# Reordering the prologue of a decoder-trunk kernel: condition weights in four staging places, three first row tiles' products beside them

## The chip, the cores and the metric

The kernel runs on one core of a Trainium2 chip. The metric is the device time of one execution in microseconds; lower is better. It is given as the median of several runs. One execution was also recorded by the hardware profiler, and every row shown below comes from that one.

## What is computed

One inference step of a one-layer decoder trunk, for 1024 prompt tokens and 8 sample tokens, width 1024. What matters here is the beginning:

```python
mod = (silu(c) @ w_ada + b_ada)              # six shifts, scales and gates per batch row
h = rmsnorm(x, g_mix) * (1.0 + sc_m) + sh_m  # needs scale and shift of mod
z = h @ w_in                                 # 256 + 4*768 columns: u | q | k | v | gate
```

Behind it stand causal pooling over u, multi-scale retention over six heads of q, k, v, an output projection, a gated MLP with a short convolution, and a final norm. All data are float32.

## The kernel before

**Tiles.** The 1024 channels lie in 8 blocks of 128 partitions (index k or j). The 1032 tokens lie in the free dimension and are cut into three row tiles c = 0, 1, 2 of 384, 384 and 264 columns (the last holds the eight samples). The normed and modulated input h is kept as a pair h_hi, h_lo, and each w_in column block as a pair hi, lo, so that one block product takes three matmuls for each k: 24 for all eight.

**The prologue** is made of small named operations, and ORDER is a list that says in which order the program emits them. An operation whose inputs have not been emitted is passed over until they are. The names:

- `L{j}{half}` loads a 512 KB block of the condition weights w_ada for channel block j (16 of them); `M{j}{half}` multiplies it by silu(c) on TensorE (four products, eight records); `F{j}` transposes the result and writes scale and shift of block j on VectorE (L257 to L263).
- `l{i}` loads the w_in column block i of the first five (q, k, v of head 0, q, k of head 1), `w{i}` splits it into hi (ScalarE, L220) and lo (VectorE or GpSimd, L221).
- `X{c}{i}` loads half of row tile c of x (that of c = 0, called x0 in the text, is loaded ahead of the list); `q{c}{k}` squares block k, with the sum `s{c}{k}` onto acc (L502); `S{c}` adds over partitions on TensorE (L302) and takes the power -1/2 on GpSimd (L292), `r{c}` spreads it over the partitions (L311) and copies it to R (L319).
- `h{c}{k}` modulates block k of row tile c: a product on VectorE (L366), or on ScalarE and GpSimd (L363, L364), then h_hi on ScalarE (L367) and h_lo on VectorE (L368). `hs` does it for the samples (L375 to L380).
- `p{c}{k}` adds block k's share to the row tile's products z in PSUM (L339 to L341): five column blocks for c = 0, two for c = 1.
- `i` begins the stream of the later weights through a ring of three raw buffers, which l0 to l4 also use.

ENG says for each such name which engine does it (0 VectorE, 1 GpSimd, for squares 2 ScalarE). A load without a place of its own in `spots` uses the raw ring: before, that is j = 5. Three staging places of two blocks each lie in memory that the h tiles of row tiles 1 and 2 use later; j = 3, 6 follow j = 0 in the first, 4 and 7 follow 1 in the second, and 2 has the third.

All these loads are issued by SyncE, one queue in order: a load that waits for its buffer holds up those behind it. The framework that builds the program puts the instructions of each engine in order itself and starts from the list's order; each engine then runs its own in order.

**After the prologue** the main loop goes through the remaining products of the input projection. Its first one, v of head 0 for row tile 1, needs a PSUM bank that the evacuation of q (head 0, row tile 0; L595 to L597) sets free, as all eight are taken.

Of the kernel before, what the change touches and what calls it, by code (L numbers as in the profile page):

```python
# [11 lines left out]
F32 = mybir.dt.float32  # L12
# [5 lines left out]
P = 128  # L18
D = 1024
KT = D // P  # L20
# [11 lines left out]
LEN = (384, 384, 264)  # L32
# [49 lines left out]

ENG = {'w3': 0, 's23': 0, 'q21': 0, 's02': 0, 's27': 0, 's12': 1, 'q20': 2, 'q12': 0, 'w2': 0, 's22': 0, 's20': 0, 't02': 1, 'q01': 2, 's17': 0, 'q13': 2, 'e': 2, 'q15': 1, 's24': 1, 's03': 0, 's16': 1, 'q05': 1, 's11': 0, 's21': 1, 't05': 0, 's15': 1, 't15': 1, 's25': 1, 'q27': 1, 'q07': 2, 't21': 1, 'q24': 2, 't16': 1, 'q10': 2, 's14': 1, 'q06': 2, 's05': 1, 't10': 0, 's06': 0, 'q26': 0, 'q11': 1, 'q04': 0, 'q00': 2, 'q02': 2, 's10': 0, 't17': 1, 's04': 1, 'q17': 2, 't13': 0, 's07': 1, 'q25': 1, 'q14': 2, 'q22': 2, 'q23': 0, 'q16': 2, 's13': 0, 't06': 0, 'q03': 2, 's26': 0, 's01': 1, 't20': 0, 'w0': 0, 't03': 0, 't24': 0, 't22': 1, 't26': 1, 'w1': 1, 's00': 0}
ORDER = """
q00 q05 l0 p00 l1 L10 L01 L00 L11 p03 q02 q03 M31 L21 l2 p04 q01 r0 h13 q07
q06 h01 S0 L20 l3 l4 X11 X10 L50 M01 p01 q15 S1 w1 L31 h26 q12 w0 M11 h25
M00 F5 L40 F0 q16 h24 L41 q04 i w2 L30 L51 q14 h00 w3 F2 M10 F1 M20 h02
M21 F3 w4 p10 p02 M30 q13 M50 M51 q21 M71 M40 q22 q11 p12 q10 h23 L60 q17 X20  # L90
h07 L61 h03 M70 p15 h15 p13 q20 M41 p11 X21 M61 h14 h20 L70 p14 h05 F4 q26 r1
M60 L71 h10 h17 h06 p05 q23 r2 p17 h04 F6 q24 h11 h22 S2 F7 q25 h16 h12 q27
p06 p16 h27 p07 hs h21
""".split()


# [33 lines left out]
def trunk_step(  # L130
# [40 lines left out]
    act = rights.enter_context(tc.tile_pool(name="act", bufs=1, side="right", reuse_waits="tile"))  # L171
# [3 lines left out]
    def big(name, dt=F32):  # L175
        return tp.tile([P, TS], dt, tag="t", name=name)

    def bank(name):
        return pg.tile([P, 512], F32, tag="g", name=name)
# [18 lines left out]
    def chunk_tile(c, tag, name, dt=F32):  # L198
        return act.tile([P, KT, LEN[c]], dt, tag=f"{tag}{c}", name=f"{name}{c}")
# [8 lines left out]
    def load_raw(src, name, raw=None):  # L208
        if raw is None:
            raw = wp.tile([P, 1024], F32, tag="raw", name=f"raw_{name}", bufs=NRAW)  # L210
        if isinstance(src, list):
            for i, part in enumerate(src):
                nc.sync.dma_start(raw[:, i * 512:(i + 1) * 512].rearrange("p (k c) -> p k c", k=2), part)
        else:
            nc.sync.dma_start(raw, src)
        return raw
# [119 lines left out]
    def gemm_k(ps, n, w, k, xh, xl, first, last):  # L336
        hi, lo = w
        ws = slice(k * P, (k + 1) * P)
        mm(ps[:, 0:n], hi[:, ws], xh[:, k, 0:n], start=first, stop=False)  # L339
        mm(ps[:, 0:n], hi[:, ws], xl[:, k, 0:n], start=False, stop=False)  # L340
        mm(ps[:, 0:n], lo[:, ws], xh[:, k, 0:n], start=False, stop=last)  # L341

    def gemm(ps, n, w, xh, xl):
        for k in range(KT):
            gemm_k(ps, n, w, k, xh, xl, k == 0, k == KT - 1)
# [10 lines left out]
    hh = [chunk_tile(0, "hh", "h_hi", F32R)]  # L356
    hl = [chunk_tile(0, "hl", "h_lo", F32R)]

    def modulate(dh, dl, src, c, k, R, scale, shift, name, spread=False):
        np_ = PLEN[c]  # L360
        t = big(name)[:, 0:np_]
        if spread:
            nc.scalar.activation(t, src[c][:, k, 0:np_], AF.Copy, scale=scale[:, k, 0:1])  # L363
            nc.gpsimd.tensor_tensor(t, t, R[:, 0:np_], op=ALU.mult)  # L364
        else:
            nc.vector.scalar_tensor_tensor(t, src[c][:, k, 0:np_], scale[:, k, 0:1], R[:, 0:np_], ALU.mult, ALU.mult)  # L366
        nc.scalar.activation(dh[c][:, k, 0:np_], t, AF.Identity, bias=shift[:, k, 0:1])  # L367
        nc.vector.scalar_tensor_tensor(  # L368
            dl[c][:, k, 0:np_], t, shift[:, k, 0:1], dh[c][:, k, 0:np_].bitcast(F32), ALU.add, ALU.subtract)
# [23 lines left out]
    for bi in range(len(in_blocks)):  # L393
        if bi < HEADS:
            for _ in range(2 if bi == 0 else 6):
                p, j, half = todo.pop(0)
# [7 lines left out]
    ready = {}  # L404
# [16 lines left out]
    def weight(key):  # L421
        while key not in ready:
            split_next()
        return ready[key]


    first = [m for (_, _, m) in in_blocks[0] + in_blocks[1]][0:NFIRST]
    early = (first, first[0:ENG.get("e", 1)])
    stage = [act.tile([P, 2, 1024], F32, tag=t, name=f"stage_{t}") for t in ("hh2", "hl2", "hl1")]
    spots = {0: stage[0], 1: stage[1], 2: stage[2], 3: stage[0], 4: stage[1], 6: stage[0], 7: stage[1]}  # L430
    ada_raw, ada_bank = {}, {}
    zps = {}
    R1, acc1, part1 = {}, {}, {}

    ops = {}
    DVE, GPS = nc.vector, nc.gpsimd
    on = lambda name, default: (DVE, GPS)[ENG.get(name, default)]

    def def_load(j, half):
        def fn():  # L440
            spot = spots[j][:, half] if j in spots else None
            ada_raw[j, half] = load_raw(w_ada[2 * j + half], f"ada0_{j}_{half}", spot)
        prev = [i for i in spots if i < j and spots[i] is spots.get(j)]
        ops[f"L{j}{half}"] = [f"M{i}{half}" for i in prev], fn

    def def_mm(j, half):
        def fn():
# [14 lines left out]
    for j in range(KT):  # L462
        for half in range(2):
            def_load(j, half)
            def_mm(j, half)
        def_fin(j)
# [20 lines left out]
    def def_sq(c, k):  # L487
        n = LEN[c]

        def fn():  # L490
# [3 lines left out]
            else:  # L494
                d = big(f"sq1_{c}_{k}")[:, 0:n]
            e = ENG.get(f"q{c}{k}", 2)
            if e == 2:
# [10 lines left out]
    def def_h(c, k):  # L508
        def fn():
            while len(hh) <= c:  # L510
                hh.append(chunk_tile(len(hh), "hh", "h_hi", F32R))
                hl.append(chunk_tile(len(hl), "hl", "h_lo", F32R))
            if ENG.get(f"t{c}{k}"):
                modulate(hh, hl, xt, c, k, R1[c], scale1, sh_m, f"h1t{c}_{k}", True)
            else:
                modulate(hh, hl, xt, c, k, R1[c], scale1, sh_m, f"h1t{c}_{k}")
        deps = [f"F{k}", f"r{c}"]
        if c == 1:
            deps += ["M20", "M21"]
        if c == 2:  # L520
            deps += ["M70", "M71", "M60", "M61", "h10"]
        ops[f"h{c}{k}"] = deps, fn

    def def_part(c, k):
        def fn():
            for m in early[c]:
                if (m, c) not in zps:
                    zps[m, c] = bank(f"z{m}_{c}")
                gemm_k(zps[m, c], LEN[c], ready["in", m], k, hh[c], hl[c], k == 0, k == KT - 1)
        deps = [f"h{c}{k}"] + [f"w{i}" for i in range(len(early[c]))]  # L530
        if k == KT - 1:
            deps += [f"p{c}{i}" for i in range(KT - 1)]
        elif k:
            deps.append(f"p{c}0")
        ops[f"p{c}{k}"] = deps, fn

    def set_acc(c):
        part1[c] = rms_a(acc1[c], c, "n1")
# [4 lines left out]
    for c in range(3):  # L543
        if c:
            def_x(c)
        for k in range(KT):
            def_sq(c, k)
            def_h(c, k)
            if c < 2 and early[c]:
                def_part(c, k)  # L550
        ops[f"S{c}"] = [f"q{c}{k}" for k in range(KT)], lambda c=c: set_acc(c)
        ops[f"r{c}"] = (f"S{c}",), lambda c=c: set_R(c)
# [5 lines left out]
    while todo_ops:  # L558
        name = next(n for n in todo_ops if all(d in done for d in ops[n][0]))
# [283 lines left out]
    for bi, blk in enumerate(in_blocks):  # L843
        g = 0
        if bi == len(in_blocks) - 1:
# [12 lines left out]
            w0 = e1p.tile([P, 2, 1024], F32R, tag="e", name="w_o0")  # L858
            split2(w0, raw)
            wo = {0: [(w0[:, 0, i * 512:(i + 1) * 512], w0[:, 1, i * 512:(i + 1) * 512]) for i in range(2)]}  # L860
        for c in range(3):
            for kind, i, m in blk:
# [3 lines left out]
                if new:  # L866
                    w = weight(("in", m))
# [381 lines left out]
    for i, (m, t) in enumerate(tail):  # L1249
# [3 lines left out]
        if i < NLEAD:  # L1253
            f = FSEQ[i]
# [43 lines left out]
    for k in (4, 5, 6, 7, 0, 1, 2, 3):  # L1298
# [7 lines left out]
        else:  # L1306
            h11, h12, h22 = x2[k, 0], x2[k, 1], x2[k + 4, 1]
# [172 lines left out]
    for p, (wn, bn) in enumerate(OUT_PRODS[:-1]):  # L1480
        ps = [banks(f"o{p}_{m}") for m in range(4)]
        st = None
        for k in range(FH - NLATE):
# [4 lines left out]
            if (p, k) in XLOADS:  # L1488
                m, t = XLOADS[p, k]
# [147 lines left out]
```

## Time and profile before

| | |
|---|---|
| median of three runs | 1235.36 us (1233.45 to 1235.67) |
| profiled execution, its own time | 1235.19 us |
| its span, first to last instruction | 1233.4 us |
| mean granted clock of TensorE | 0.986 of full speed |
| TensorE busy | 1196.7 us (97%) |
| VectorE, ScalarE, GpSimd busy | 845.4, 487.6, 402.2 us |
| warm-up products on TensorE end | 13.47 us |
| first product of the main loop starts | 75.24 us |

A matmul is recorded with a modelled end, so consecutive ones overlap; their pace is read from start to start. The granted clock is 1.0 at 2.4 GHz and 0.5 at 1.2 GHz. Times within the span are counted from its first instruction.

### The profile page before, as it was taken

The page shows a single profiled execution, that of the slowest core. Times are in us where ns is not written, and L with a number is a line of the kernel's source. Part 1 is how long each engine was busy: PE and PEld are TensorE (multiplying, and loading weights), DVE is VectorE, ACT ScalarE, POOL GpSimd, SP SyncE. Part 2 cuts the span into 40 slices and gives each one's busy share as a digit, 9 for nine tenths or more (in the row PEclk, how much of TensorE's full clock was granted, in tenths as well). Part 3 has the DMA queues.
Part 4 walks back from the last instruction along what each step waited for, and adds up shares of the span by engine and source line. Part 5 has one row for each costly group of instructions (what it writes and reads, how often), then busy time and mean ns, then how long its engine had stood idle before and what let it go on. Part 6 is the DMA issues. An engine that isn't in the chain of part 4 may idle for free.

```text
span 1233.4 us, 23770 instructions
## 1 busy us (share of the span) xinstructions
PE 1196.7 (97%) x9376; PEld 1161.6 (94%) x9376; DVE 845.4 (69%) x1558; ACT 487.6 (40%) x970; POOL 402.2 (33%) x375
## 2 busy tenths in 40 slices
PE   8999999999999999979999999999999999999996
PEld 6788999999999999979999999999999999999996
DVE  4775565555672452579988888778787778768662
ACT  3463342443421432345333333333333465543532
POOL 3541121111140011105656545454636315140114
PEclk8999999999999999989999999999999999999998
DMA  8814454453530173211323232322322599865513
GB/s 308 303 56 162 130 168 126 122 169 118 166 90 3 64 254 105 69 60 35 120 104 112 94 105 104 103 78 103 107 100 96 155 299 315 284 187 168 177 41 134
DMA packets 97087, 169.53 MB, mean 137 GB/s; under 512 B 13296, under 2 KB 46288, under 8 KB 96976
## 3 DMA queue, kind: packets, MB, share of 16 engines
q1 hardware_dynamic: 93632, 167.07, 41.3%
q8 instruction: 74, 1.21, 0.4%
q10 hardware_dynamic: 3344, 0.95, 0.3%
q14 instruction: 37, 0.30, 0.1%
HBM read 135.26 MB, written 32.73 MB: 136 GB/s over the span
## 4 chain that ended last, share of the span: by engine, by line
PE 77%; DVE 12%; DMA 5%; issue 2%; ACT 1%; POOL 1%; SPq 0%; DVEq 0%; POOLq 0%; ACTq 0%
PE z L339 8%; PE z L341 7%; PE z L340 7%; PE pS L955 6%; PE pS L957 6%; PE pS L956 6%; PE pA L955 5%; PE pA L957 5%; PE pA L956 5%; PE o L1397 2%; PE o L1399 2%; PE o L1398 2%; DVE o L828 2%; PE mo L955 2%; PE mo L957 2%; PE mo L956 2%
## 5 line engine op out<-in xcount | busy, mean ns | idle before, releaser
L339 PE MATMUL z<-h_hi,hi_in 128*128 128x384 f32 (+1 forms) x624 | 203.9, 329 | 1.2 <-DVE qT L597 0.6
L340 PE MATMUL z<-h_lo,hi_in 128*128 128x384 f32 (+1 forms) x624 | 199.1, 319 | 0.2 <-DVE h_lo L368 0.2
L341 PE MATMUL z<-h_hi,lo_in 128*128 128x384 f32 (+1 forms) x624 | 198.3, 318 | 0.1
L1397 PE MATMUL o<-o 128*128 128x258 f32 x616 | 175.6, 285 | 5.8 <-DVE xs L1411 2.7
L1398 PE MATMUL o<-o 128*128 128x258 f32 x616 | 173.9, 282 | 0.0
L1399 PE MATMUL o<-o 128*128 128x258 f32 x616 | 173.7, 282 | 0.0
L955 PE MATMUL pS<-T,w_S 128*128 128x258 f32 x528 | 150.3, 285 | 2.1 <-DVE u_lead L1127 1.1
L956 PE MATMUL pS<-T,w_S 128*128 128x258 f32 x528 | 149.6, 283 | 0.4 <-DVE T L828 0.4
L957 PE MATMUL pS<-T,w_S 128*128 128x258 f32 x528 | 149.5, 283 | 0.0
L339 PEld LDWEIGHTS z<-h_hi,hi_in 128*128 128x128 f32 x624 | 117.3, 188 | 15.8 <-issue 13.2
L1397 PEld LDWEIGHTS o<-o 128*128 128x128 f32 x616 | 116.4, 189 | 7.4 <-DVE xs L1411 3.4
L340 PEld LDWEIGHTS z<-h_lo,hi_in 128*128 128x128 f32 x624 | 117.7, 189 | 1.3 <-DVE h_lo L368 0.9
L341 PEld LDWEIGHTS z<-h_hi,lo_in 128*128 128x128 f32 x624 | 117.2, 188 | 0.4 <-DVE lo_in L221 0.4
L1398 PEld LDWEIGHTS o<-o 128*128 128x128 f32 x616 | 116.9, 190 | 0.0
L1173 POOL TENSOR_TENSOR mix_all<-mix_all 128x516 f32<-128x516 f32 x44 | 64.8, 1474 | 159.2 <-DVE mix_all L1127 134.2
L1399 PEld LDWEIGHTS o<-o 128*128 128x128 f32 x616 | 116.6, 189 | 0.0
L828 DVE SCALAR_TENSOR_TENSOR o<-raw_o,o 128x516 fp32r<-128x516 f32 (+1 forms) x132 | 96.3, 764 | 24.4 <-ACT o L831 23.9
L831 ACT CAST o<-raw_o 128x516 fp32r<-128x516 f32 (+1 forms) x132 | 77.3, 621 | 85.7 <-PE o L1399 40.6
L955 PEld LDWEIGHTS pS<-T,w_S 128*128 128x128 f32 x528 | 100.4, 190 | 3.0 <-DVE mix_all L1127 1.4
L956 PEld LDWEIGHTS pS<-T,w_S 128*128 128x128 f32 x528 | 100.4, 190 | 0.6 <-DVE T L828 0.6
L957 PEld LDWEIGHTS pS<-T,w_S 128*128 128x128 f32 x528 | 100.6, 190 | 0.0
L831 ACT CAST w_S<-S 128x512 fp32r<-128x512 f32 x88 | 54.3, 620 | 114.0 <-PE pS L957 65.5
(265 smaller groups left out, 3227.6 us busy)
## 6 DMA issues: line engine op xcount, KB each, us to landing
fd<-mix_all SPq DMA_DIRECT2D x77, 258.0 KB, 2.6
raw_o<-fd SPq DMA_DIRECT2D x77, 258.0 KB, 4.0
raw_o<-w_fout SPq DMA_DIRECT2D x77, 256.0 KB, 4.3
raw_ada<-w_ada SPq DMA_DIRECT2D x64, 256.0 KB, 3.6
raw_in<-w_in SPq DMA_DIRECT2D x26, 512.0 KB, 4.4
raw_a<-w_fin SPq DMA_DIRECT2D x25, 512.0 KB, 3.8
raw_b<-w_fin SPq DMA_DIRECT2D x22, 512.0 KB, 3.5
x2d<-mix_all SPq DMA_DIRECT2D x16, 258.0 KB, 2.3
```

Of the source, the lines that this page charges most:

```text
L339: mm(ps[:, 0:n], hi[:, ws], xh[:, k, 0:n], start=first, stop=False)
L340: mm(ps[:, 0:n], hi[:, ws], xl[:, k, 0:n], start=False, stop=False)
L341: mm(ps[:, 0:n], lo[:, ws], xh[:, k, 0:n], start=False, stop=last)
L828: nc.vector.scalar_tensor_tensor(dst, a, 1.0, b, ALU.mult, ALU.subtract)
L831: nc.scalar.copy(dst[:, 0], src)
L955: mm(o, w[0][:, ks], b[:, 0, cols], start=first and kk == 0, stop=False)
L956: mm(o, w[0][:, ks], b[:, 1, cols], start=False, stop=False)
L957: mm(o, w[1][:, ks], b[:, 0, cols], start=False, stop=end)
L1173: nc.gpsimd.tensor_tensor(s, s, Bt.pop((f, t)), op=ALU.mult)
L1397: mm(o, w[:, 0, ms_], b[:, 0, cols], start=first, stop=False)
L1398: mm(o, w[:, 0, ms_], b[:, 1, cols], start=False, stop=False)
L1399: mm(o, w[:, 1, ms_], b[:, 0, cols], start=False, stop=last)
```

## The change

ORDER is written anew: the condition weights' loads, products and ends go k by k, with h and p of row tile 0 two blocks behind; then row tile 1; row tile 2 stands last. Four staging places instead of three (the fourth in the memory of row tile 1's h_hi) take block j in place j modulo 4, so L4 to L7 wait for M0 to M3 and no condition weight goes through the raw ring. Of the five products of row tile 0, three are still made k by k beside the condition weights; the other two become operations of their own, `b0` and `b1`, 24 matmuls each. All squares of row tile 0 go to ScalarE, its sums and all five splits to VectorE; block 5's product with R goes to ScalarE and GpSimd as block 2's does. Row tile 1's h waits for M6 and M7, row tile 2's for M4 and M5, whose places they overwrite.

```diff
--- before.py
+++ after.py
@@ -82,15 +82,13 @@
 
 
 
-ENG = {'w3': 0, 's23': 0, 'q21': 0, 's02': 0, 's27': 0, 's12': 1, 'q20': 2, 'q12': 0, 'w2': 0, 's22': 0, 's20': 0, 't02': 1, 'q01': 2, 's17': 0, 'q13': 2, 'e': 2, 'q15': 1, 's24': 1, 's03': 0, 's16': 1, 'q05': 1, 's11': 0, 's21': 1, 't05': 0, 's15': 1, 't15': 1, 's25': 1, 'q27': 1, 'q07': 2, 't21': 1, 'q24': 2, 't16': 1, 'q10': 2, 's14': 1, 'q06': 2, 's05': 1, 't10': 0, 's06': 0, 'q26': 0, 'q11': 1, 'q04': 0, 'q00': 2, 'q02': 2, 's10': 0, 't17': 1, 's04': 1, 'q17': 2, 't13': 0, 's07': 1, 'q25': 1, 'q14': 2, 'q22': 2, 'q23': 0, 'q16': 2, 's13': 0, 't06': 0, 'q03': 2, 's26': 0, 's01': 1, 't20': 0, 'w0': 0, 't03': 0, 't24': 0, 't22': 1, 't26': 1, 'w1': 1, 's00': 0}
+ENG = {'s23': 0, 'q21': 0, 's27': 0, 's12': 1, 'q20': 2, 'q12': 0, 's22': 0, 's20': 0, 's17': 0, 'q13': 2, 'e': 2, 'q15': 1, 's24': 1, 's16': 1, 's11': 0, 's21': 1, 's15': 1, 't15': 1, 's25': 1, 'q27': 1, 't21': 1, 'q24': 2, 't16': 1, 'q10': 2, 's14': 1, 't10': 0, 'q26': 0, 'q11': 1, 's10': 0, 't17': 1, 'q17': 2, 't13': 0, 'q25': 1, 'q14': 2, 'q22': 2, 'q23': 0, 'q16': 2, 's13': 0, 's26': 0, 't20': 0, 't24': 0, 't22': 1, 't26': 1, 'q00': 2, 'q01': 2, 'q02': 2, 'q03': 2, 'q04': 2, 'q05': 2, 'q06': 2, 'q07': 2, 's01': 0, 's02': 0, 's03': 0, 's04': 0, 's05': 0, 's06': 0, 's07': 0, 't02': 1, 't05': 1, 'w0': 0, 'w1': 0, 'w2': 0, 'w3': 0, 'w4': 0}
 ORDER = """
-q00 q05 l0 p00 l1 L10 L01 L00 L11 p03 q02 q03 M31 L21 l2 p04 q01 r0 h13 q07
-q06 h01 S0 L20 l3 l4 X11 X10 L50 M01 p01 q15 S1 w1 L31 h26 q12 w0 M11 h25
-M00 F5 L40 F0 q16 h24 L41 q04 i w2 L30 L51 q14 h00 w3 F2 M10 F1 M20 h02
-M21 F3 w4 p10 p02 M30 q13 M50 M51 q21 M71 M40 q22 q11 p12 q10 h23 L60 q17 X20
-h07 L61 h03 M70 p15 h15 p13 q20 M41 p11 X21 M61 h14 h20 L70 p14 h05 F4 q26 r1
-M60 L71 h10 h17 h06 p05 q23 r2 p17 h04 F6 q24 h11 h22 S2 F7 q25 h16 h12 q27
-p06 p16 h27 p07 hs h21
+q00 q01 q02 q03 q04 q05 q06 q07 S0 l0 L00 L01 l1 L10 L11 l2 L20 L21 w0 M00 M01 F0 L30 L31 r0 w1
+M10 M11 h00 F1 L40 L41 w2 M20 M21 h01 p00 F2 L50 L51 M30 M31 h02 p01 F3 L60 L61 M40 M41 h03 p02 F4
+L70 L71 M50 M51 h04 p03 F5 l3 X10 X11 l4 M60 M61 h05 p04 F6 w3 M70 M71 h06 p05 F7 w4 h07 p06 p07
+X20 X21 q10 q11 q12 q13 b0 q14 q15 q16 q17 S1 r1 b1 h10 p10 h11 p11 h12 p12 h13 p13 h14 p14 h15 p15
+h16 p16 h17 p17 q20 q21 q22 q23 q24 q25 q26 q27 S2 r2 i h20 h21 h22 h23 h24 h25 h26 h27 hs
 """.split()
 
 
@@ -425,9 +423,9 @@
 
 
     first = [m for (_, _, m) in in_blocks[0] + in_blocks[1]][0:NFIRST]
-    early = (first, first[0:ENG.get("e", 1)])
-    stage = [act.tile([P, 2, 1024], F32, tag=t, name=f"stage_{t}") for t in ("hh2", "hl2", "hl1")]
-    spots = {0: stage[0], 1: stage[1], 2: stage[2], 3: stage[0], 4: stage[1], 6: stage[0], 7: stage[1]}
+    early = (first[0:3], first[0:ENG.get("e", 1)])
+    stage = [act.tile([P, 2, 1024], F32, tag=t, name=f"stage_{t}") for t in ("hh2", "hl2", "hl1", "hh1")]
+    spots = {j: stage[j % 4] for j in range(KT)}
     ada_raw, ada_bank = {}, {}
     zps = {}
     R1, acc1, part1 = {}, {}, {}
@@ -440,8 +438,7 @@
         def fn():
             spot = spots[j][:, half] if j in spots else None
             ada_raw[j, half] = load_raw(w_ada[2 * j + half], f"ada0_{j}_{half}", spot)
-        prev = [i for i in spots if i < j and spots[i] is spots.get(j)]
-        ops[f"L{j}{half}"] = [f"M{i}{half}" for i in prev], fn
+        ops[f"L{j}{half}"] = [f"M{j - 4}{half}"] if j >= 4 else [], fn
 
     def def_mm(j, half):
         def fn():
@@ -516,9 +513,9 @@
                 modulate(hh, hl, xt, c, k, R1[c], scale1, sh_m, f"h1t{c}_{k}")
         deps = [f"F{k}", f"r{c}"]
         if c == 1:
-            deps += ["M20", "M21"]
+            deps += ["M60", "M61", "M70", "M71"]
         if c == 2:
-            deps += ["M70", "M71", "M60", "M61", "h10"]
+            deps += ["M40", "M41", "M50", "M51", "h10"]
         ops[f"h{c}{k}"] = deps, fn
 
     def def_part(c, k):
@@ -533,6 +530,16 @@
         elif k:
             deps.append(f"p{c}0")
         ops[f"p{c}{k}"] = deps, fn
+
+
+    def def_rest(i, m):
+        def fn():
+            zps[m, 0] = bank(f"z{m}_0")
+            gemm(zps[m, 0], LEN[0], ready["in", m], hh[0], hl[0])
+        ops[f"b{i}"] = [f"w{i + 3}"] + [f"h0{k}" for k in range(KT)], fn
+
+    for i, m in enumerate(first[3:]):
+        def_rest(i, m)
 
     def set_acc(c):
         part1[c] = rms_a(acc1[c], c, "n1")
```

## Rows read from the trace of the kernel before

**Rows 1.** Busy time by stretch (first line: the columns)

```profile
core 0: us, PE busy (x) PEld busy (x) DVE busy (x) ACT busy (x) POOL busy (x), PEclk, DMA share, GB/s
13.50:75.20 61.70, 53.20 (x364) 41.18 (x364) 46.02 (x90) 27.79 (x58) 26.88 (x25) 0.92 0.67 236
3.00:25.00 22.00, 17.73 (x132) 14.57 (x132) 7.01 (x12) 6.50 (x13) 8.92 (x7) 0.86 1.04 399
25.00:29.00 4.00, 4.00 (x24) 2.20 (x24) 3.37 (x7) 2.82 (x5) 0.00 (x0) 0.51 0.12 43
```

**Rows 2.** SyncE's queue in order of time: start, duration, line, what

```profile
9.13 0.33 SPq L215 DMA_DIRECT2D stage_hl<-w_ada  x1
15.91 1.88 SPq L215 DMA_DIRECT2D raw_in<-w_in  x2
...
28.45 0.34 SPq L215 DMA_DIRECT2D raw_ada<-w_ada  x1
...
41.25 1.69 SPq L215 DMA_DIRECT2D stage_hl<-w_ada  x2
```

**Rows 3.** TensorE in order of time; in brackets the idle time before

```profile
1.08 12.39 PE L195 MATMUL warm<-ones 128*128 128x128 f32 x92 [1.08 <-DVE ones L192]
14.37 1.07 PE L243 MATMUL ada_ps<-stage_hh,cs 128*32 128x256 f32 x16 [0.90 <-DMA stage_hh<-w_ada]
18.34 1.18 PE L302 MATMUL ss_n<-ones,acc 128*128 128x2 f32 x6 [2.90 <-POOL acc L502]
...
25.36 1.93 PE L243 MATMUL ada_ps<-stage_hl,cs 128*32 128x256 f32 x16
...
62.90 0.80 PE L302 MATMUL ss_n<-ones,acc 128*128 128x2 f32 x6 [1.75 <-DVE hs L375]
...
67.54 0.33 PE L341 MATMUL z<-h_hi,lo_in 128*128 128x384 f32 x1
...
73.26 0.34 PE L341 MATMUL z<-h_hi,lo_in 128*128 128x384 f32 x1
...
75.24 0.44 PE L339 MATMUL z<-h_hi,hi_in 128*128 128x384 f32 x1 [0.64 <-DVE qT L597]
```

**Rows 4.** VectorE in order of time, end of the prologue

```profile
62.68 0.21 DVE L375 TENSOR_TENSOR hs<-x_all,scale 128x64 f32<-128x64 f32 x1
...
65.00 0.24 DVE L1560 COPY cvs<-scv 128x176 f32<-128x176 f32 x1
67.36 1.76 DVE L366 SCALAR_TENSOR_TENSOR h1t<-x_all,scale,R_n 128x256 f32<-128x256 f32 x3 [2.12 <-ACT R_n L319]
...
74.63 0.56 DVE L597 TENSOR_TENSOR qT<-z,rope 128x384 f32<-128x384 f32 x1
```

**Rows 5.** ScalarE in order of time, squares of row tile 0

```profile
7.86 0.94 ACT L498 ACTIVATE sq<-x_all 128x384 f32<-128x384 f32 x2 [0.63 <-DMA x_all<-x]
```

**Rows 6.** GpSimd in order of time

```profile
31.74 1.81 POOL L500 TENSOR_TENSOR sq<-x_all 128x384 f32<-128x384 f32 x1
...
55.11 0.89 POOL L502 TENSOR_TENSOR acc<-acc,sq 128x264 f32<-128x264 f32 x1 [5.91 <-ACT sq L498]
```

**Rows 7.** GpSimd by line and shape to 74 us: busy, mean ns

```profile
L502 POOL TENSOR_TENSOR acc<-acc,sq 128x384 f32<-128x384 f32 x8 | 9.1, 1142 | 2.6 <-ACT hi_in L220 1.7 <-DVE acc L502 0.5
```

**Rows 8.** VectorE by line and shape to 75 us: busy, mean ns

```profile
L368 DVE SCALAR_TENSOR_TENSOR h_lo<-h1t,modT,h_hi 128x384 fp32r<-128x384 f32 x16 | 9.8, 644 | 0.1
L366 DVE SCALAR_TENSOR_TENSOR h1t<-x_all,scale,R_n 128x384 f32<-128x384 f32 x12 | 9.0, 775 | 1.0 <-ACT R_n L319 1.0
L502 DVE TENSOR_TENSOR acc<-acc,sq 128x384 f32<-128x384 f32 x6 | 5.5, 914 | 11.6 <-POOL acc L502 11.4
...
L368 DVE SCALAR_TENSOR_TENSOR h_lo<-h1t,modT,h_hi 128x256 fp32r<-128x256 f32 x8 | 3.4, 475 | 0.0
L366 DVE SCALAR_TENSOR_TENSOR h1t<-x_all,scale,R_n 128x256 f32<-128x256 f32 x5 | 3.1, 670 | 2.1 <-ACT R_n L319 2.1
...
L377 DVE TENSOR_TENSOR hs<-hs,R_n 128x64 f32<-128x64 f32 x1 | 0.8, 757 | 0.0
```

## The prediction

> **What bounds the kernel now.** Four views were read, in this order. The windows of the prologue come first: from the end of the warm-up products at 13.5 us to the first product of the main loop at 75.2 us TensorE is busy 53.2 us of 61.7, so it idles 8.5 us, and its granted clock is 0.92 of full speed, which costs at most another 0.08 x 61.7 = 4.9 us [rows 1]. So the prologue holds 61.7 - 8.5 - 4.9 = 48.3 us of TensorE work at 2.4 GHz; the change can touch only the rest, 13.4 us, about 1% of the span. After 75.2 us nothing is edited, so the prediction is the new start of that first product, and everything behind it moves with it.
>
> The second view is the order of SyncE's queue. The transfers run at 399 GB/s from 3 to 25 us and at 43 GB/s from 25 to 29 us [rows 1]. The reader is to see why: SyncE issues the eleventh load at 9.13, the fourth and fifth w_in columns (l3, l4) only at 15.91 when GpSimd has split a raw block, and L50 at 28.45, when VectorE has split another; L50 lies in the raw ring, and every load behind it waits in line. The last condition weights (L70, L71) are issued at 41.25 [rows 2].
>
> The third view is TensorE in order of time. M0 starts at 14.37, S0 at 18.34 after 2.90 us of idle, waiting for GpSimd's sum; sixteen M records take 1.07 us before that and 1.93 us at 25.36, which is the low clock after the idle stretch. S2 runs at 62.90; the first main-loop product starts at 75.24 and waits for VectorE's evacuation of a bank [rows 3].
>
> The fourth is VectorE: the tail of the prologue is its work. From row tile 2's factor (R2, first use 67.36) to that evacuation (74.63) it has h2 to write and hardly a gap [rows 4]. So in the last stage VectorE ends last, not TensorE; the change pays by what it takes out of that tail or lets start earlier.
>
> **The change part by part.**
>
> *Loads.* All sixteen L blocks now have a staging place, none goes through the raw ring; the fourth place is the memory of row tile 1's h_hi. New waits: L4 to L7 wait for M0 to M3, and SyncE issues nothing behind them (l3, X1, l4, X2, the stream) until then. Calibration: M0 started at 14.37 when x0 (1.57 MB), the parameters (0.21) and five blocks of 0.524 MB, 4.41 MB, were ahead of it; 4.41/0.399 = 11.05, so landing = 3.3 us + MB/0.399. Then L01 (3.35 MB) lands at 11.7, L11 at 15.6, L21 at 19.6, L31 (7.55 MB) at 22.2, L71 (11.74 MB) at 32.7, X10 at 36.0, X11 (13.84 MB) at 38.0. M0 can run at 14.3, 8 us before the queue would run dry, so these waits cost nothing; without that cover each microsecond late is a microsecond on X11. X1, however, is moved behind ten L blocks: before, its squares began at 31.74 [rows 6], now they begin at 36.0.
>
> A page speaks against these times: the Trainium skill, "DMA: Bandwidth & Descriptors", section "Where 436 GB/s comes from", holds that loads from HBM are bound near 358 GB/s for a core. By it X11 would come at 3.3 + 13.84/0.358 = 42.0 and the sum below would end 4.0 us later, at 1231; the 399 GB/s of [rows 1] disagree, and the sum goes by them.
>
> *Row tile 0's statistics.* The eight squares go to ScalarE, the seven sums to VectorE. The second half of x lands at 7.86 and two squares take 0.94 us [rows 5]: four end at 9.8, the sums at about 11. SyncE and TensorE are not touched; TensorE's warm-up ends at 13.47, so S0 runs at 13.5 instead of 18.34, 4.8 us earlier. Four sums and one split move from GpSimd to VectorE, at most 4 x 0.91 + 1.3 = 5.0 us, hidden by VectorE's idle time before 20 us (7.0 us busy in the 22 us to 25 us [rows 1]); were that cover gone, 5 us of h0 would come later, in a stretch that has slack until R1.
>
> *TensorE's order.* The work is the same (two of five row-tile-0 products become blocks of 24 matmuls). One matmul every (73.26 - 67.54)/33 = 0.173 us [rows 3] makes b0 and b1 4.2 us each and p0k 1.56 us. With the 48.3 us from above and no idle time the stage would end at 13.5 + 48.3 = 61.8. M7 cannot come before 32.7 us; up to then there is 8.6 us of M and about five p0k to run, so TensorE has gaps early but not after 21 us. b1 stands between S1 and p10 and covers the wait for R1.
>
> *Row tile 1's statistics,* the new critical piece. From 36.0: three sums on VectorE (mean 0.91 us [rows 8]), four on GpSimd (mean 1.14 us [rows 7]) and two squares there, in one chain, 3 x 0.91 + 6 x 1.14 = 9.6 us, so S1 at 45.6. Before, the same chain ran from 31.74 to S1 at 41.15 by the same engines, 9.4 us, which agrees. Lower bound: unhampered, some 8 us, 44.0. From S to the first use of R took 67.36 - 62.90 = 4.5 us [rows 3, 4]. So h10 starts at 50.1 (48.0 to 51.5).
>
> *VectorE behind it.* h1: 8 h_lo of 0.61 us and 5 products of 0.75 (busy time over count) make 8.6 us; h2: 3.4 + 3.1 = 6.5; the samples 0.8 + 3 x 0.2 = 1.4 [rows 8]. Sum 16.5 us, if h0, all F and the sums of row tile 2 are done before R1, between 39 and 50 us, when VectorE has little else. Before, the same tail held four more h0, their F and the wait for R2, and ended at 74.63 [rows 4]; now it ends at 50.1 + 16.5 = 66.6. Lower: TensorE's own bound, 61.8. Upper: 51.5 + 16.5 + 4.4 (all seven squares and sums of row tile 2 that VectorE has, at 0.91 x 264/384) = 72.4. I take 66.6, as the rows used were measured with GpSimd active as it will be. Gain 74.63 - 66.6 = 8.0 us (2.2 to 12.8).
>
> Staging costs nothing at the end: h1 overwrites the places of M2, M3, M6 and M7 (about 36 us), 14 us before h10. h2 needs M4 and M5, long done. l4, needed by b1, lands at 39.4.
>
> **The rivals.**
>
> *Row tile 2 comes last (slower).* The new list puts all of its squares behind p17. If they also stand there in VectorE's queue, its chain starts at 50.1 + 8.6 = 58.7 and takes 9.6 x 264/384 = 6.6 us, R2 follows 4.5 later at 69.8, and h2 takes the 7.3 us from 67.36 to 74.63: 77.1, 2.5 us later than now. TensorE would then idle some 12 us; after 2.9 us of idle it fell to 1.2 GHz and lost up to 4.9 us [rows 1, 3]. Together 1237.7 to 1242.6. It decides as soon as S2 comes behind h17. For it: GpSimd's sum at 55.11 waited 5.91 us for a square placed late [rows 6]. Against it: engines don't follow the list literally; VectorE ran the samples' first step (second last in the list) at 62.68 and a copy from the very end of the program at 65.00 [rows 4], so ready work is pulled into gaps.
>
> *TensorE comes late.* If M6 and M7 stand ahead of the products in its queue, or short bursts of M between loads let the clock fall, p0 runs only after 32.7: 168 matmuls x 0.173 = 29.1 and some 4 us of statistics end at 66, with 4.9 us of low clock at 71: 1231.5. For it: the drop at 18.34 [rows 3]. Against it: the gaps here are below 2 us, and 1.75 us of idle at 62.90 was followed by full rate.
> The Trainium skill, "TensorE: Matmul & The Clock Gate", section "HAM oscillation — how this bites in real kernels", describes just this, bursts shorter than the wait for the next load that run slow each time. By that rule the time is the 1231.5 of this rival; before, the trace agrees only at the drop after 2.90 us.
>
> *Given back later.* The prologue ends 8 us earlier and the first block's evacuations wait for rope tables or raw blocks that come no earlier: 1235. Against it: those loads follow X2 (42 us) in line, some 9 us of transfer, so about 51 us, ahead of 66.
>
> **How the numbers follow.** The profiled execution took 1235.19 us (span 1233.4 and 1.8 around it); the median of the runs is 1235.36, so the two may be used alike. 1235.2 - 8.0 = 1227.2, rounded to 1227; this case's own range is 1222 to 1233, chance 0.60. Row tile 2 last: 0.17. TensorE late: 0.13. Given back: 0.10. A measurement of this kernel tells about 0.2%, 2.5 us, from no change. Faster: 0.58 of the first case and nearly all of TensorE late, 0.69; same: 0.02 + 0.10 + 0.02 and a little of row tile 2 last, 0.15; slower 0.16. The range reaches from 1221 to 1238: it leaves out some 0.07 below and 0.13 above.
>
> **What would show it.** S0 at 13.5; no hole in the transfers before 41 us; L70 issued before 27; S1 near 45.6; h10's product near 50; S2 before h17; the first main-loop product near 67. Wrong if S2 comes after 58 us, if the clock is low past 30 us, or if that product starts near 67 and the span is still 1233.

## The result, and the profile after

The changed kernel takes 1244.66 us (median, 1244.12 to 1247.78) against 1235.51 us (1233.45 to 1236.03) for the kernel before in the same series: ratio 1.0082, interval 1.0062 to 1.0103, so 9 us slower. The prediction was 1227, in a range from 1221 to 1238. It was wrong, and on the other side.

The windows of the changed kernel, columns as in [rows 1]:

```profile
13.50:82.76 69.26, 53.72 (x361) 40.54 (x361) 37.50 (x81) 26.61 (x54) 21.67 (x22) 0.88 0.57 203
3.00:25.00 22.00, 19.49 (x175) 15.96 (x175) 12.01 (x26) 10.05 (x19) 1.95 (x2) 1.00 1.04 404
25.00:29.00 4.00, 3.62 (x30) 2.20 (x29) 1.80 (x5) 0.92 (x3) 0.89 (x1) 1.00 1.03 410
60.00:80.00 20.00, 15.10 (x89) 13.49 (x87) 12.02 (x24) 7.88 (x17) 9.87 (x11) 0.82 0.07 12
```

The front does what was forecast: 404 GB/s up to 25 us, 410 where the kernel before had its hole of 43 [rows 1], and full clock. But TensorE's 53.7 us of busy time now fill 69.3 us instead of 61.7, and between 60 and 80 us it idles 4.9 us and runs at 0.82 of the clock. TensorE in order of time says what it waited for:

```profile
13.11 0.73 PE L300 MATMUL ss_n<-ones,acc 128*128 128x2 f32 x6
...
52.38 1.41 PE L300 MATMUL ss_n<-ones,acc 128*128 128x2 f32 x6 [2.57 <-DVE acc L499]
...
55.91 1.65 PE L309 MATMUL ss_n<-co,rsr_n 128*128 128x128 f32 x6 [1.27 <-POOL rsr_n L290]
...
73.70 1.41 PE L300 MATMUL ss_n<-ones,acc 128*128 128x2 f32 x6 [3.19 <-DVE acc L499]
76.30 1.22 PE L309 MATMUL ss_n<-co,rsr_n 128*128 128x128 f32 x4 [1.19 <-POOL rsr_n L290]
...
78.27 1.93 PE L241 MATMUL ada_ps<-raw_ada,cs 128*32 128x256 f32 x16 [0.51 <-ACT R_n L317]
82.76 0.69 PE L337 MATMUL z<-h_hi,hi_in 128*128 128x384 f32 x1 [2.56 <-ACT ada_sb L274]
...
91.56 0.46 PE L629 MATMUL ra<-qT,kT 128*128 128x128 f32 x2 [2.66 <-DVE kT L606]
```

In the kernel before (TensorE, ScalarE, SyncE's queue):

```profile
41.15 0.83 PE L302 MATMUL ss_n<-ones,acc 128*128 128x2 f32 x6
...
66.94 0.38 ACT L319 COPY R_n<-ss_n 128x264 f32<-128x264 f32 x1 [3.63 <-PE ss_n L313]
...
55.34 6.15 SPq L568 DMA_DIRECT2D rope<-rope  x6
...
79.51 0.38 PE L622 MATMUL ra<-qT,kT 128*128 128x128 f32 x2
```

S0 comes at 13.11 (before 18.34), but S1 at 52.38 (before 41.15, forecast 45.6) and S2 at 73.70, 10.8 us later than in [rows 3]. The main loop's first product is 7.5 us late (82.76 against 75.24). The first product of the attention, which the kernel before ran at 79.51, is 12 us late. From there to 480 us the shift of the two traces stays near 11.3 us; the kernel before then has a stretch of low clock that the changed one lacks (588.7 to 592.1 us), and 9.4 us are left at the end. So the loss is made before 92 us. ScalarE in order of time shows where the squares stand:

```profile
43.47 0.61 ACT L365 ACTIVATE h_hi<-h1t,modT 128x384 fp32r<-128x384 f32 x1 [1.04 <-DVE h1t L364]
43.99 0.51 ACT L495 ACTIVATE acc<-x_all 128x384 f32<-128x384 f32 x1
...
57.60 0.48 ACT L317 COPY R_n<-ss_n 128x384 f32<-128x384 f32 x1 [10.50 <-PE ss_n L309]
...
65.27 0.41 ACT L495 ACTIVATE acc<-x_all 128x264 f32<-128x264 f32 x1
...
77.83 0.38 ACT L317 COPY R_n<-ss_n 128x264 f32<-128x264 f32 x1 [9.34 <-PE ss_n L311]
```

And GpSimd, VectorE:

```profile
36.96 0.83 POOL L497 TENSOR_TENSOR sq<-x_all 128x384 f32<-128x384 f32 x1
...
64.94 0.43 DVE L497 TENSOR_TENSOR sq<-x_all 128x264 f32<-128x264 f32 x1
```

Row tile 1's x had landed by 36.96, when GpSimd squared a part of it. ScalarE's first square of that tile runs at 43.99, directly behind h07's h_hi. Row tile 2's first squares run at 64.94 (VectorE) and 65.27 (ScalarE), among the last h1 parts, although ScalarE stood idle 10.5 us ahead of R1's copy. The tail of VectorE, to be laid beside [rows 4], and SyncE's queue:

```profile
72.65 0.90 DVE L499 TENSOR_TENSOR acc<-acc,sq 128x264 f32<-128x264 f32 x2 [1.57 <-POOL acc L499]
...
78.25 0.48 DVE L364 SCALAR_TENSOR_TENSOR h1t<-x_all,scale,R_n 128x256 f32<-128x256 f32 x1 [2.94 <-ACT R_n L317]
...
87.19 0.56 DVE L604 TENSOR_TENSOR qT<-z,rope 128x384 f32<-128x384 f32 x1 [1.74 <-DMA rope<-rope]
```

```profile
24.46 2.14 SPq L213 DMA_DIRECT2D stage_hh<-w_ada  x2
...
27.13 0.97 SPq L480 DMA_DIRECT2D x_all<-x  x2
...
79.41 2.51 SPq L211 DMA_DIRECT2D raw_ada<-w_ada  x4
82.02 3.23 SPq L575 DMA_DIRECT2D rope<-rope  x6
```

Behind h2 a second wait has appeared: the first evacuation (the step that takes the finished q out of PSUM) waits 1.74 us for the rope tables, by which it multiplies q and k. They are issued at 82.02, behind raw blocks that SyncE could issue only after TensorE's products of 78.27; the kernel before issued them at 55.34.

### The profile page after: what moved, and what is told of

Read it like the earlier page. It is cut to its first block, busy times and chain, and to the rows that moved or that the text cites. A ratio compares the mean times of both kernels' runs of the same rounds, so it can differ in the third digit from the quotient of the medians.

```text
span 1242.8 us, 23769 instructions
## 1 busy us (share of the span) xinstructions
PE 1196.9 (96%) x9376; PEld 1160.7 (93%) x9376; DVE 847.5 (68%) x1561; ACT 489.0 (39%) x973; POOL 393.1 (32%) x370
## 4 chain that ended last, share of the span: by engine, by line
PE 79%; DVE 10%; DMA 4%; POOL 2%; issue 2%; ACT 2%; SPq 0%; DVEq 0%; POOLq 0%; ACTq 0%
PE z L337 8%; PE z L338 7%; PE z L339 7%; PE pS L962 6%; PE pS L964 6%; PE pS L963 6%; PE pA L962 5%; PE pA L964 5%; PE pA L963 5%; PE o L1404 3%; PE o L1406 3%; PE o L1405 3%; PE mo L962 2%; PE mo L963 2%; PE mo L964 2%
```

## The experiments

Sixteen kernels were run. The table gives for the profiled execution of each the times (us) of S1, of R2's copy on ScalarE, of the first q evacuation and of the first attention product; then the median and the ratio to the kernel before in the same series (its medians: 1234.2 to 1235.5). Where a run's list is printed below, it is cut to the places that bear on the text.

```
run                              S1    R2     q     att    median  ratio, interval
before                          41.2  66.9  74.6   79.5   1235.5
after                           52.4  77.8  87.2   91.6   1244.7  1.0082 1.0062-1.0103
1  row tile 2 early             53.1  68.4  81.3   85.4   1241.3  1.0048 1.0030-1.0067
2  row tile 1 early             42.8  75.1  84.6   88.9   1243.8  1.0065 1.0044-1.0086
3  rope early                   53.7  78.1  85.8   89.9   1243.5  1.0069 1.0046-1.0091
4  loads alone                  40.0  65.9  73.6   78.3   1234.9  1.0001 0.9987-1.0015
5  TensorE kept busy            53.9  75.9  85.4   89.8   1244.9  1.0084 1.0065-1.0104
6  before, row tile 2 last      40.9  74.4  83.3   87.7   1244.0  1.0078 1.0054-1.0102
7  1 + 2 + 3                    42.1  71.3  83.6   87.8   1242.8  1.0066 1.0048-1.0084
8  spread                       47.2  67.2  79.9   83.9   1240.9  1.0048 1.0030-1.0066
9  loads and row tile 0         38.5  67.5  75.1   79.8   1234.5  0.9988 0.9979-0.9997
10 9 and two whole products     43.7  74.6  83.5   88.7   1243.2  1.0064 1.0044-1.0083
11 woven                        44.5  69.3  81.7   88.2   1243.7  1.0074 1.0052-1.0097
12 1, r2 behind h17             52.9  71.6  80.7   86.8   1241.4  1.0050 1.0036-1.0064
13 8, r2 behind h17             46.2  68.7  76.3   80.4   1237.4  1.0019 1.0008-1.0030
14 11, r2 behind h17            44.5  72.8  80.5   85.4   1242.0  1.0058 1.0037-1.0078
15 12 and rope early            56.5  75.4  83.1   87.2   1242.0  1.0052 1.0032-1.0073
16 13, rope late                47.0  70.3  79.8   84.5   1240.5  1.0052 1.0032-1.0073
```

The first four columns come from one execution each, the medians from 4 to 12. Executions of one kernel differ by up to 10 us (run 14: 1238.5 to 1248.7), and the profiled one need not lie near the median (run 1's, 1245.56, is the slowest of its ten). Still the columns carry the medians: the median less the time of the first attention product is 1153 to 1157 us in all eighteen rows, while that product itself moves from 78.3 to 91.6. Runs 7, 8, 10 and 11 came out slower than either of the two ranges that had been expected of them.

**One part of the change undone (1 to 3).** Run 1 moves row tile 2's statistics forward:

```diff
 S1
+q20 q21 q22 q23 q24 q25 q26 q27
 r1 b1 h10 p10 h11 p11 h12 p12 h13 p13
+S2 r2
 h14 p14 h15 p15 h16 p16 h17 p17
-q20 q21 q22 q23 q24 q25 q26 q27 S2 r2
 i h20 h21 h22 h23 h24 h25 h26 h27 hs
```

> The changed kernel, but row tile 2's squares and sums stand behind S1 in the list and S2, r2 before h14, instead of behind p17. Theory A (the list's place of row tile 2's statistics sets when the engines do them, and that makes TensorE idle from 70 to 83 us): S2 moves from 73.7 to about 62 to 66 us, h2 follows h1 without a gap, the first main-loop product starts near 74 to 76 instead of 82.8, and the time falls by 7 to 11 us to 1234 to 1238. Rival B (the loss is row tile 1, whose load stands behind ten more weight blocks): S2 moves, but at most 2 us are won, 1242 to 1245. Rival C (the rope tables are late): 1242 or more, as these do not move.

Run 2 moves row tile 1's load and statistics:

```diff
 F0 L30 L31
+X10 X11
 r0
...
 M60 M61
+q10 q11 q12 q13 q14 q15 q16 q17 S1 r1
 h05 p04 F6
```

> The changed kernel, but row tile 1's load stands behind L31 and its squares, S1 and r1 before h05. Theory A with B as a second, separate loss: TensorE's gap and slow stretch between 49.5 and 58 us go (about 7 us), S1 moves from 52.4 to about 38 to 41; row tile 2 stays last and TensorE still idles between p17 and the main loop: 1235 to 1239. If row tile 2 alone were the loss: 1243 to 1246, the wait before it only gets longer. If B alone were the loss: 1231 to 1234, as before.

Run 3 issues the rope loads directly behind X21; nothing else is edited:

```diff
 X20 X21
+R
```

> The changed kernel, but the six rope loads are issued behind X2 instead of behind the stream's second pair of condition weights. Theory A: the evacuation of q waits 1.7 us for the rope table at 87 us, so 1 to 4 us are won, 1240.5 to 1243.5. Rival C (the rope tables hold the end of the prologue): 5 us or more, below 1239.5. No effect: 1244 to 1245.

None brings the 9 us back. Against 1244.66 they are 3.3, 0.8 and 1.1 us faster; the last two lie within the width of the intervals, so that runs 2 and 3 by themselves show no gain. Run 1 has R2 9.4 us earlier, but only 5.9 of it is left at q's evacuation.

**What is innocent (4 and 5).** Run 4 is the kernel before with the four staging places and the waits that come with them; list, engines and the five products k by k as before:

```diff
-stage = [act.tile([P, 2, 1024], F32, tag=t, name=f"stage_{t}") for t in ("hh2", "hl2", "hl1")]
-spots = {0: stage[0], 1: stage[1], 2: stage[2], 3: stage[0], 4: stage[1], 6: stage[0], 7: stage[1]}
+stage = [act.tile([P, 2, 1024], F32, tag=t, name=f"stage_{t}") for t in ("hh2", "hl2", "hl1", "hh1")]
+spots = {j: stage[j % 4] for j in range(KT)}
```

> The list, the engines and the five products of the kernel before, with only the four staging places of the changed kernel and their waits. Theory A (the loss is the order of the list, not the loads): 1231 to 1236, as L5 no longer waits in the raw ring for a split. Rival D (the new waits of L4 to L7 for M0 to M3 hold up SyncE's queue): 1238 or more.

Run 5 is the changed kernel with 28 further products ahead of S1 and of S2, into columns of the bank that nothing reads, so that TensorE does not idle there:

```diff
+        if name == "n1" and c:
+            w = hh[c - 1][:, KT - 1, 0:P]
+            for _ in range(NKEEP):
+                mm(ps[:, 384:496], w, w[:, 0:112], start=True, stop=True)
```

> The changed kernel with 28 extra products (of h, into unused columns, results not read) ahead of S1 and 28 ahead of S2 on TensorE, in its two idle stretches; they add work only there. If the fall to 1.2 GHz is a cost of its own (theory A's second part), the granted clock stays at 1.0 and 2 to 5 us are won, 1239.5 to 1242.5. If the clock is only a symptom and the end is set by the statistics of row tiles 1 and 2: 1243.5 to 1246.

The loads cost nothing and bring nothing that can be measured (1.0001). The kept-busy run loses the first of the two stretches of low clock (the changed kernel has 1.2 GHz from 52.4 to 59.2 and from 72.8 to 86.5 us; here only from 75.6 to 85.8), and its time is that of the changed kernel. So this first stretch is not what costs the 9 us. The second stayed in run 5; but in runs 14 and 15 the clock is full from 59.2 and 65.1 us to beyond 500 us, and their attention still begins at 85.4 and 87.2, their medians 1242.0. So the low clock here follows from the waits; as a cost by itself it does not show.

**The rival by itself (6).** The kernel before, every operation in its own order, with only row tile 2's squares, S2, r2 and what needs R2 moved behind the last p1 and p0:

```diff
-S1 X20 L61 h03 p03 q20 q21 q22 M41 X21
+S1 X20 L61 h03 p03 M41 X21
...
-h07 h17 q25 h16 h12 p12 q27 S2 r2 h26 h25 h24 h23 h20 h22 p06 p16 p17 h27 p07 hs h21
+h07 h17 h16 h12 p12 p06 p16 p17 p07
+q20 q21 q22 q26 q23 q24 q25 q27 S2 r2 h26 h25 h24 h23 h20 h22 h27 hs h21
```

> The kernel before, with one thing of the change alone: squares, S2, r2 and h of row tile 2 stand behind p17 and p07 in its list. Theory A (this place alone costs what the change lost in its second stretch): S2 moves from 62.9 to about 71 to 74 us, TensorE idles some 10 us, 1241 to 1247. If the loss needs the new staging or the k-by-k front as well: 1234 to 1237.

It takes 1243.95 us: this one move, with p06, p16, p17 and p07 now ahead of h2, makes the kernel before 9.6 us slower, as much as the whole change. TensorE and SyncE's queue in it:

```profile
71.52 0.80 PE L300 MATMUL ss_n<-ones,acc 128*128 128x2 f32 x6 [1.09 <-DVE acc L500]
73.51 0.71 PE L309 MATMUL ss_n<-co,rsr_n 128*128 128x128 f32 x4 [1.19 <-POOL rsr_n L290]
...
77.91 0.69 PE L337 MATMUL z<-h_hi,hi_in 128*128 128x384 f32 x1 [1.73 <-ACT ada_sb L274]
...
87.67 0.46 PE L620 MATMUL ra<-qT,kT 128*128 128x128 f32 x2 [3.30 <-DVE kT L597]
```

```profile
75.52 2.51 SPq L211 DMA_DIRECT2D raw_ada<-w_ada  x4
78.14 3.00 SPq L566 DMA_DIRECT2D rope<-rope  x6
```

S2 is 8.6 us late, and the rope tables have slid behind the raw blocks here too, though nobody moved them.

**Why undoing it gave so little back (7, 8, 11 to 14).** Run 7 joins runs 1, 2 and 3, with row tile 2's squares placed only ahead of h10. Run 8 spreads the statistics (against the changed kernel):

```diff
 h07
+S1 r1
 p06 p07 X20 X21
+R q20 q21 q22 q23 q24 q25 q26 q27
 b0 b1 h10 p10 h11 p11 h12 p12
+S2 r2
 h13 p13 h14 p14 h15 p15 h16 p16 h17 p17
```

(row tile 1's load and squares as in run 2).

> The changed kernel with all three moves together: row tile 1's load behind L31 and its statistics before h05, row tile 2's squares before h10 and S2, r2 before h14, rope loads behind X2. Theory A (two idle stretches of TensorE in series, both made by the list): both go, the main loop begins at 66 to 71 us, 1228 to 1233. If the k-by-k front itself costs (TensorE's changes between M, F and p): 1235 to 1240.

> The same three moves, but S1 and r1 only before p06, row tile 2's squares before b0 and S2, r2 before h13, so that no engine meets a wait for the factor R1 before it has finished h06. Theory A: main loop at 64 to 69 us, 1226 to 1232. If the k-by-k front itself costs: 1235 to 1240, as in the run with the three moves.

In run 8 S2 comes at 64.05, R2 as early as in the kernel before, and the time is still 1240.9. ScalarE shows why:

```profile
61.17 0.62 ACT L365 ACTIVATE h_hi<-h1t,modT 128x384 fp32r<-128x384 f32 x1 [2.89 <-DVE h1t L364]
67.19 0.38 ACT L317 COPY R_n<-ss_n 128x264 f32<-128x264 f32 x1 [5.41 <-PE ss_n L311]
67.47 0.62 ACT L361 ACTIVATE h1t<-x_all,scale 128x384 f32<-128x384 f32 x1
67.98 1.83 ACT L365 ACTIVATE h_hi<-h1t,modT 128x384 fp32r<-128x384 f32 x3
```

R2's copy waits 5.41 us for TensorE, and the remaining 128x384 pieces of h1, which do not need it, stand behind it in ScalarE's queue. The same holds in run 1 (r2 ahead of h14), in run 7, and in run 11, which weaves h1 among the last h0 (against run 8):

```diff
-h05 p04 F6 w3 M70 M71 h06 p05 F7 w4 h07 S1 r1 p06 p07
+M60 M61 M70 M71 F6 F7 S1 h05 p04 r1 w3 X20 X21 R w4 h06 p05 h10 h07 p06 h11 p10
...
+h12 p11 h13 p12 S2 b0 r2 h14 p13 h15 p14 b1 h16 p15 h17 p16 p17
```

> The changed kernel with row tiles 1 and 2 spread and, unlike the run with the tiles spread (1240.9), the row tile 1 parts h1 and p1 woven among the last h0 and p0, with M6 and M7 ahead of h05, row tile 2's sum in the middle of h1 and the two whole products behind it. If the 5 us that the spread version still lost come from h1 and h2 standing in line behind all h0 (theory 1, second half): 1233 to 1237. If they come from the front taken k by k, which this keeps up to h04 (theory 2): 1239 to 1243. A new wait, M6 and M7 ahead of h05 in the queue of TensorE before their weights have landed, would show as idle time of TensorE near 37 to 43 us and cost 1 to 3 us.

The table's columns R2 and q say it for all runs. From R2's copy to q's evacuation it is 7.7 us in the kernel before, 12.4 to 12.9 in the four runs with R2's copy ahead of h1 parts (1, 7, 8, 11), 7.6 to 7.7 in runs 3, 4, 9, 13, 14 and 15, and 8.9 to 9.5 in the changed kernel and the rest; in these, run 10 apart, the rope tables were issued only after 74 us. Runs 12 to 14 move r2 alone behind h17 in runs 1, 8 and 11 (in the last, w3, w4 and the two whole products too); run 13's edit:

```diff
-S2 r2
+S2
 h13 p13 h14 p14 h15 p15 h16 p16 h17
+r2
 p17
```

> The run with row tile 2's squares early (1241.3) with one further move: r2, and with it the copy of R2 on ScalarE, behind h17 instead of ahead of h14; S2 stays ahead of h14. Theory 1 (R2's copy in ScalarE's queue held h14 to h17, whose data were ready): the main loop starts 1 to 3 us earlier and the time is 1237.5 to 1240. Theory 2 (the remaining loss lies in the front and in S1, which this does not touch): 1240.5 to 1242.

> The version with row tiles 1 and 2 spread (1240.9) with r2 alone moved behind h17; S2 stays ahead of h13. Theory 1: h13 to h17 no longer wait for R2 (R2's copy stood at 67.2 ahead of them), VectorE's two idle stretches of 2.4 and 1.6 us between 62 and 68 us go, 1236 to 1239. Theory 2: 1240 to 1242.

> The woven version (1243.7) with r2, w3, w4 and both whole products behind h17, so that neither R2's copy (6.9 us of idle time on ScalarE there) nor the splits of the fourth and fifth columns stand ahead of h1. Theory 1: 1234 to 1238, the level of the kernel before. Theory 2: 1240 to 1243. A third way: with the two whole products at the end, TensorE runs 8.4 us of them after h1 and they end last; then the first evacuation waits for them and the time is 1237 to 1240.

From R2's copy to q it is 7.6 us now in runs 13 and 14. Run 13 is within 2.4 us of the kernel before: 7 of the 9 us are back. As it keeps the front taken k by k and the two whole products, these cost no more than the 2.4 us that are left, unless a gain elsewhere hides more. In run 14 r2 ran only at 72.02, since the list put b0 and most of p1 ahead of it in TensorE's queue. Run 12's time did not move at all. In its trace VectorE's second step of q waits for GpSimd, and GpSimd for the rope tables, issued at 75.89:

```profile
84.03 1.33 DVE L606 TENSOR_TENSOR qT<-qT,rt_q 128x384 f32<-128x384 f32 x1 [2.73 <-POOL rt_q L605]
```

**The next wait (15 and 16).** Run 12 has rope and row tile 1 late. Run 15 is run 12 with the rope loads as in run 3; run 16 is run 13 with them put back:

```diff
 X20 X21
-R
 q20 q21 q22 q23 q24 q25 q26 q27
```

> The run with row tile 2 early and r2 behind h17 (1241.4), with the six rope loads issued right behind row tile 2's x instead of behind the stream's first blocks; row tile 1 stays late. If the late rope tables hold the first evacuations (q's second step waited 2.7 us, the first product of the attention came 6 to 8 us late though the main loop's first product came only 1.3 us late): 1236 to 1239. If row tile 1's statistics at 52.9 are what holds it: 1240 to 1242.

> The spread version with r2 behind h17 (1237.4), with the rope loads put back to the place that the change gives them, behind the stream's first raw blocks. If the rope tables are the new wait: back to 1240 to 1242, with q's first evacuation waiting for a transfer. If not: 1237 to 1238.5.

SyncE's queue, VectorE and TensorE in run 16:

```profile
74.61 2.98 SPq L575 DMA_DIRECT2D rope<-rope  x6
```

```profile
79.76 0.56 DVE L604 TENSOR_TENSOR qT<-z,rope 128x384 f32<-128x384 f32 x1 [1.84 <-DMA rope<-rope]
```

```profile
75.22 0.44 PE L337 MATMUL z<-h_hi,hi_in 128*128 128x384 f32 x1 [2.86 <-ACT ada_sb L274]
...
84.47 0.77 PE L629 MATMUL ra<-qT,kT 128*128 128x128 f32 x2 [4.81 <-DVE kT L606]
```

Its main loop starts at 75.22, within 0.02 us of where it started in the kernel before, and then the rope tables, issued at 74.61, hold the evacuation; the attention begins 5 us late and the clock is low from 83.8 to 90.6 us. 1240.5 against 1237.4: with the statistics repaired, the late rope loads cost 3 us, while ahead of that repair moving them gave nothing that can be measured (run 3). Not all of it is shown to be the wait for the tables. Of the 3.5 us by which q is later than in run 13 (76.28) that wait is 1.84; R2's copy was already 1.6 us later. The built order differs there too: VectorE's short step between S2 and r2 (L302; the first row is run 13, the second run 16) stands behind h17 in run 16.

```profile
63.99 0.15 DVE L302 TENSOR_SCALAR rsv_n<-ss_n 128x3 f32<-128x3 f32 x1
...
68.22 0.15 DVE L302 TENSOR_SCALAR rsv_n<-ss_n 128x3 f32<-128x3 f32 x1
```

Run 15 cannot tell whether row tile 1's late statistics cost anything by themselves: VectorE's order came out another way, with three squares and at least one sum of row tile 2 ahead of the last sum of row tile 1, and S1 fell from 52.9 to 56.5.

**The rest of the change in the kernel before (9 and 10).** Run 9 is run 4 with row tile 0's statistics as in the change; run 10 adds the two whole products:

```diff
+q00 q01 q02 q03 q04 q05 q06 q07 S0
 l0 l1 L10 L01 L00 L11 L21 l2
...
```

```diff
-    early = (first, first[0:ENG.get("e", 1)])
+    early = (first[0:3], first[0:ENG.get("e", 1)])
...
-h16 h12 q27 p06 p16
+h16 h12 b0 q27 p06 b1 p16
```

> The kernel before with the four staging places (as in the run with the loads alone, 1234.9) and, on top of that, row tile 0's statistics as in the changed kernel: eight squares on ScalarE, seven sums on VectorE, S0 first in the list. Row tiles 1 and 2 keep the places that they had before. Theory 1 (the loss comes from where the statistics of row tiles 1 and 2 stand): S0 at 13.1 to 13.8 instead of 18.4, the end of the prologue 0 to 4 us earlier, 1231 to 1235. Theory 2 (the front of the new list costs about 5 us by itself, which is why moving the statistics forward within it gave back only 3 to 4 us): 1237 to 1240.

> The kernel of the run before it in this call with one thing more from the change: three first products k by k and two whole, the first of the two ahead of row tile 2's last square, the other behind p06. Theory 1: the two blocks of 24 products stand in the tail where TensorE waited, so not slower than the run with the early statistics, 1228 to 1235. Theory 2 (two products whole leave VectorE and ScalarE less cover in the front): 1237 to 1241.

Run 9 has S0 at 13.71 and ends 1 us ahead of the kernel before (0.9988): 4.7 us at S0 are worth about 1 us at the end (0.4 to 2.6 by the interval). It is the best version seen, by less than the 0.2% named in the prediction, and its trace does not show where the 1 us comes from: q's evacuation is no earlier (75.1 against 74.6). Run 10 is 9 us slower than run 9. Its trace shows that b0 and several p1 stood ahead of S2 in TensorE's queue (VectorE's last sum for S2 began at 62.52, S2 at 71.83), and that TensorE had less to do while the condition weights came (columns as in [rows 1]):

```profile
20.00:40.00 20.00, 14.24 (x81) 8.57 (x82) 9.38 (x18) 8.27 (x15) 5.28 (x6) 0.83 0.98 369
```

TensorE is busy 14.2 of 20 us there (before 19.3). That three products instead of five are the reason is not shown: the changed kernel has three as well and is busy 18.9 us. So run 10 says that these places for the blocks are bad, not that whole products are.

## Why the prediction was wrong, step by step

**Loads: right.** L70 was issued at 24.46, no hole before 41 us, row tile 1's x there by 37. The 358 GB/s that the Trainium skill gives as a bound in "DMA: Bandwidth & Descriptors", section "Where 436 GB/s comes from", did not show: 404 and 410 GB/s. Run 4 shows that the four places alone bring nothing that can be measured.

**Row tile 0's statistics: right in time** (13.11 for 13.5), and worth about 1 us (run 9). **TensorE's order: right** for the front (18.9 us busy of 20 from 20 to 40 us, full clock), so *TensorE comes late* is out; its clock fell only at 52.4 us, behind 2.57 us of waiting for S1, as a follower (runs 5, 14 and 15).

**Row tile 1's statistics: the length was right, the start wrong.** From ScalarE's first square to S1 it is 52.38 - 43.99 = 8.4 us, forecast 9.6. But the chain was started at 36.0, when x lands; it started at 43.99, where the list has it, behind h07. The kernel before had shown the same (SyncE's queue, a window with columns as in [rows 1], GpSimd):

```profile
17.84 0.98 SPq L483 DMA_DIRECT2D x_all<-x  x2
...
27.00:28.00 1.00, 1.00 (x6) 0.78 (x3) 1.00 (x2) 0.68 (x2) 0.00 (x0) 0.50 0.00 0
...
30.38 1.40 POOL L364 TENSOR_TENSOR h1t<-h1t,R_n 128x384 f32<-128x384 f32 x1 [9.72 <-ACT h1t L363]
```

Row tile 1's x was issued there at 17.84, and between 27 and 28 us nothing moved (0 GB/s), so it had landed; GpSimd stood idle 9.72 us and yet squared it only at 31.74, behind block 2's product [rows 6]. That 31.74 was a place in a queue, not a landing, and the forecast set a landing, 36.0, beside it.

**VectorE behind it: this is the step that failed.** The 16.5 us of tail stood on the condition that the sums of row tile 2 are done before R1, in time when VectorE has little else. They were done at 73.6, behind all of h1, so the tail became h1, the sums, S2 to R2 (4.1 us), h2. Worked with the measured start: R1's first use 58.11, h1 to 68.6, the sums 5, R2 4.1, then the 7.7 us from R2 to q and 1.7 for the rope tables give 87.1; the evacuation ran at 87.19. Of the 20.6 us between this and the forecast 66.6, about 8.0 are R1's later start, 1.9 the longer h1, 9.1 the sums and R2, 1.7 the rope tables. R1's start alone put right brought nothing that can be measured (run 2), as h2 waits for R2.

**The rival *Row tile 2 comes last* is what happened,** and run 6 shows that it is enough by itself. Its place and condition were right (S2 behind h17). That its price, 1237.7 to 1242.6, was only 2 us short is in part luck: it started from R1 at 50.1, 8 us early, and left the rope tables out, but charged up to 4.9 us for the low clock, which does not show as a cost of its own. It was given only 0.17 because of one inference: the samples' step and a copy from the end of the program had been pulled ahead [rows 4], so ready squares would be too. They were not: in run 12 ScalarE squared the same data at 47.49, here at 65.27, where the list had them.

```profile
47.49 0.42 ACT L495 ACTIVATE acc<-x_all 128x264 f32<-128x264 f32 x1
```

The built order is not the list word for word (run 15), but readiness does not decide it either. The rows that spoke for the rival, GpSimd's 5.91 us of waiting for a square placed late and the square at 31.74 [rows 6], were the better evidence.

***Given back later* was right as a second wait.** The argument against it took the rope loads to follow X2 in line, at 51 us. They slid behind blocks that wait for TensorE (82.02). It does not decide while S2 is late; once S2 is mended the late loads take back 3 us (13 against 16), 1.84 of it shown as the wait for the tables.

Left open: the last 2 us of run 13 (1.0008 to 1.0030), what row tile 1's place costs once row tile 2's is put right, and by what rule the framework orders what is ready.

## What to carry to other kernels

A queue in order makes the place of an instruction part of its cost: when a list is rewritten, read in the built order of every engine what stands ahead of each short reduction that a whole stage waits for, and do not count on ready work being pulled forward. A wait put back in place must not stand ahead of work that does not need it (R2's copy), and DMA issues that nobody edited can slide behind a waiting one (the rope tables). Where several waits stand in a row, undoing one gives little: test each alone in the kernel before, and then together in the kernel after.

## What the runs showed of the hardware that was not expected

TensorE at 1.2 GHz for 20.5 of the 34 us from 52.4 to 86.5 us hardly shows in the time by itself: with the first 6.8 us of it gone (run 5) the ratio is 1.0084, against 1.0082, and run 15, at full clock from 65.1 us on, still begins its attention at 87.2. At the end of the second stretch TensorE waits 2.66 us for VectorE (91.56), so there the work at half the clock fitted into a wait that was there anyway.
